# A hybrid attention block on one core: the high parts of A's q are set down by transfers that ScalarE issues

## The chip, the core and the metric

The kernel runs on one core of a Trainium2 chip. The core has five engines that run side by side, each in the order of its own queue: TensorE (PE in the profile) multiplies matrices, VectorE (DVE), ScalarE (ACT) and GpSimd (POOL) work elementwise, and SyncE (SP) does nothing here but issue transfers (DMAs). SP and ACT each have a queue from which transfers can be issued; the transfers themselves run on the DMA engines. Engines wait for one another, and for transfers, on semaphores. The metric is the device time of one execution in microseconds (us); lower is better. The time quoted is the median of three runs.

## What is computed

One transformer block in float32, 1024 tokens of width 1024. Its token-mixing half, cut to what matters:

```python
proj = h @ w_in[l]
qa = partial_rope(proj[..., :o1].reshape(b, s, A_Q_HEADS, HEAD_DIM), cos, sin)
ka = partial_rope(proj[..., o1:o2].reshape(b, s, A_KV_HEADS, HEAD_DIM), cos, sin)
...
oa = banded_attention(qa.reshape(b, s, A_KV_HEADS, A_GROUP, HEAD_DIM), ka, va,
                      A_WINDOW - 1, sink=sink_a[l])
...
ob = dilated_mixture_attention(qb, kb, vb).reshape(b, s, B_W).astype(x.dtype)
mixed = jnp.concatenate([rms_norm(oa, g_mix_a[l]), rms_norm(ob, g_mix_b[l])], axis=-1)
y = mixed @ w_out[l]
```

Mixer A has 8 query heads of 64 in two groups of 4, each group with one key and one value head, a window of 128 and a sink. Mixer B has 8 heads with three dilated windows each. An MLP of width 4096 follows.

## The kernel before

Matrix products that need float32 accuracy are made from parts: a number is split into a high part (rounded to a format that TensorE takes fast) and a low part (what is left), and three products are added (lines 861, 862 and 864 for the projections). So each projection result is split after it is computed, and both parts are stored.

**Projections.** There are six groups `u`: 0 and 1 are mixer A's (4 query heads, 1 key head, 1 value head each), 2 to 5 are mixer B's. Each is computed for two halves `x` of 512 tokens and three chunks `c` of 128 columns. `evac` (lines 734 to 844) takes a finished chunk out of PSUM: ACT writes the high part into a staging tile `hl` (line 763 after the rotary embedding on DVE in lines 757 to 760, or line 774), and DVE or POOL writes the low part beside it (line 766 or 777). The columns are laid out (`PARTS_A`, `PARTS_B`) so that the rows of a chunk belong to several heads interleaved. Transfers from SBUF to SBUF then set the rows down where TensorE needs them (line 803): keys into `kt`, queries into `qt`. In mixer A the high parts of q go to partitions 0 to 63 of `qt` and the low parts to partitions 64 to 127, in separate transfers (`s_` is 0 or 1), while a transfer of k carries both parts to both places (`both`). For each of the four pairs of `u` and `x` in mixer A that is 2 transfers for k, 5 for q's high and 5 for q's low parts. In mixer B it is q whose transfers carry both parts and k that is split.

**Scores.** Mixer A's items run per block of 128 queries: line 1177 multiplies `qt` and `kt` into `s_ps`, DVE adds the mask and finds the maximum (1192), ACT takes exponentials (1197), DVE the reciprocal (1201), ACT or POOL scales the rows (1207, 1209), TensorE transposes (1234), ACT and DVE split the transposed weights (1241, 1245), TensorE multiplies by the values (1269), ACT and DVE take the result out (1304, 1309) and SP stores it (1314). The values come by `vt` (825), a transpose (831) and `v_hl` (839, 842). Between these, TensorE computes the next projections.

**Buffers.** `hl` tiles come from a ring of five staging slots, which the ada weights `wa_st` (line 994, consumed by POOL in lines 1005 to 1010) and the gates `gate_st` (1034, stored in 1050) use too. A tile in a slot is free when the last transfer that reads it has landed. Weights of the projections come by `w_st` (530) and are split by ACT (539) and DVE or POOL (544). A rope table is made through `ptab` (719) and `tab` (721).

**Order.** Nothing here is scheduled by hand in the code's text. `Sched` (lines 175 to 313) is a list scheduler that runs while the program is built: each step carries an engine, a modelled duration, dependences, buffers it takes and gives, and a priority, and the step that can start first by the model is written out next. Where a step may run on two engines (`alts`), the one that would end first by the model gets it. For transfers the model keeps one clock of the DMA engines, `dma`, and counts 0.62 us of SP's time for each issue. Its clocks are estimates; on the chip the engines keep this order but run by their semaphores. All 533 transfers are issued by SP. Each transfer signals one of eight semaphores, given out in turn in the order in which the program was written, and in the compiled order a transfer waits for the one eight before it.

Of the kernel before, what the change touches and what calls it, by code (L numbers as in the profile page):

```python
# [148 lines left out]
PW = 0.0  # L149


class Ev:

    __slots__ = ("t", "eng")
# [20 lines left out]
class Sched:  # L175


    def __init__(self):
        self.clk = dict(PE=0.0, ACT=0.0, DVE=0.0, POOL=0.0, SP=0.0)
        self.queue = {e: [] for e in ("ACT", "DVE", "POOL", "SP")}  # L180
        self.pe = {}
        self.launch = []
        self.seq = 0
        self.dma = 0.0
        self.filler = None

    def step(self, dur, emit, deps=(), takes=(), gives=(), prio=5, after=None, kind="", n=1):
# [25 lines left out]

    def ready(self, o, e):
        t = 0.0
        for d in o.deps:
            if d.t is None:
                return None
            x = d.t + lat(d.eng, e)
            if x > t:  # L220
                t = x
        for r, n in o.takes:
            if n == 0:
                continue
            if len(r.free) < n:
                return None
            x = sorted(r.free)[n - 1]
            if x > t:
                t = x
        return t  # L230

    def give_out(self, e, o, start):
        dur, emit = o.alts[e] if o.alts else (o.dur, o.emit)
        for r, n in o.takes:
            r.free.sort()
            del r.free[:n]
        emit()
        end = start + dur
        if e == "SP":
            self.clk[e] = start + 0.62 * o.n  # L240
            self.dma = max(self.dma, start + 1.1) + max(dur, 0.62 * (o.n - 1))
            end = self.dma + 0.8
        else:
            self.clk[e] = end
        o.ev.t = end
        o.ev.eng = e
        o.gone = True
        for r, n in o.gives:
            r.give(end, n, e)
        self.end = end  # L250
        if o.after:
            o.after()
# [96 lines left out]
def hybrid_block(ctx: ExitStack, tc: tile.TileContext, x, positions, w_ada, b_ada, g_attn_post, w_in, w_out,  # L349
                 g_mlp_post, w_up, w_down, consts, out):  # L350
    nc = tc.nc
    ctx.enter_context(tc.manual_schedule())
    V, A, G, T = nc.vector, nc.scalar, nc.gpsimd, nc.tensor
    x, out = x[0], out[0]
# [91 lines left out]
            return ring_r(name)  # L446
        return st.stgp.tile([P, 1024], F32, name=name, tag="stg")

    def load(emit, nbytes, deps=(), takes=(), prio=5, gives=(), after=None, n=1):
        return op("SP", nbytes / (345e3 if prio > -500 else 370e3), emit, deps, takes=takes, prio=prio, gives=gives, after=after, n=n)  # L450

    def rsqrt_mean(dst, src, dep):
        box = []
# [280 lines left out]
    def evac(u, x, c, get_ps, done, r_bank):  # L734

        isb = u > 1
        parts = (PARTS_B if isb else PARTS_A)[c]
        cs = slice(512 * x, 512 * x + 512)
        b = {}
        e_q.setdefault((u, x), [])  # L740
        e_k.setdefault((u, x), [])

        def posted():
            n_in[u, x] = n_in.get((u, x), 0) + 1
            if n_in[u, x] == 3:
                st.posted += 1

        def f_new():
            b["f"] = stage("hl")[:].rearrange("p (s t) -> p s t", s=2)
            b["t"] = b["f"].bitcast(F32R)  # L750

        if c == 0:
            def f_rope():
                f_new()
                ps, t = get_ps(), b["f"][:, 1]
                cos, sin = tabs[0][:, cs], tabs[1]
                V.tensor_tensor(t[64:128], ps[0:64], sin[0:64, cs], ALU.mult)
                V.tensor_tensor(t[0:64], ps[64:128], sin[64:128, cs], ALU.mult)
                V.tensor_tensor(ps[:], ps[:], cos, ALU.mult)
                V.tensor_tensor(t, t, ps[:], ALU.add)  # L760
            e0 = e_rot[u, x] = op("DVE", 4 * t_dv(512), f_rope, [done] + e_tab[x], takes=[(r_stg, 1)],
                                  gives=[(r_bank, 1)], prio=2)
            eh = op("ACT", t_sb(512), lambda: A.copy(b["t"][:, 0], b["f"][:, 1]), [e0], prio=2)

            def f_lo(eng):
                return lambda: eng.tensor_tensor(b["t"][:, 1], b["f"][:, 1], b["f"][:, 0], ALU.subtract)
            el = op(("DVE", "POOL"), (t_dv(512), t_ptt(512)), (f_lo(V), f_lo(G)), [eh], prio=2)
        elif parts:
            n = P if c < 2 else parts[-1][1]
            sc_ = scl[0] if isb else None  # L770

            def f_hi():
                f_new()
                A.mul(b["t"][:n, 0], get_ps()[:n], -0.125 if sc_ is None else sc_[:n])

            def f_lo():
                V.scalar_tensor_tensor(b["t"][:n, 1], get_ps()[:n], -0.125 if sc_ is None else sc_[:n],
                                       b["f"][:n, 0], ALU.mult, ALU.subtract)
            eh = op("ACT", t_ps(512) + AP_COST, f_hi, [done, e_rot[u, x]], takes=[(r_stg, 1)], prio=2)
            el = op("DVE", t_dv(512) + AP_DV, f_lo, [eh], gives=[(r_bank, 1)] if c < 2 else [], prio=2)  # L780

        if parts:
            for whose in ("k", "q") if c == 0 else ("q", "k"):
                mine = [a for a in parts if a[3] == whose]
                if not mine:
                    continue
                both = isb == (whose == "q")
                nh = 2 if isb else 4 if whose == "q" else 1
                for s_ in ((0, 1) if not both else (None,)):
                    new = c == 0 and whose == "k" and s_ in (0, None)  # L790

                    def f_st(s_=s_, new=new, mine=mine, whose=whose, nh=nh, both=both):
                        if new:
                            if not x:
                                ks[u] = kring.tile([P, 2, 1024], F32R, name="kt", tag="kt")
                            qs[u, x] = qring.tile([P, 4, 512], F32R, name="qt", tag="qt")
                        dst = qs[u, x][:] if whose == "q" else ks[u][:, :, cs]
                        for p0_, n_, step, _, row in mine:
                            src = b["f"][p0_:p0_ + (n_ - 1) * step + 1:step]
                            m_ = n_ // nh  # L800
                            for i in range(2) if both else (s_,):
                                o = dst[64 * i + row:64 * i + row + m_].bitcast(F32)
                                nc.sync.dma_start(o, src if both else src[:, s_])  # L803
                    if new:
                        e_new[u, x] = Ev()
                    last = (whose == ("q" if c == 0 or not isb else "k")) and s_ in (1, None)

                    def after(new=new, last=last):
                        if new:
                            e_new[u, x].t = 0.0  # L810
                        if last and c < 2:
                            posted()
                    by = sum(a[1] * 2048 * (4 if both else 1) for a in mine)
                    e = load(f_st, by, [eh if s_ == 0 else el] + ([] if new else [e_new[u, x]]),
                             takes=[(r_k, 1 - x), (r_q, 1)] if new else [], prio=-12, n=len(mine) * (2 if both else 1),
                             gives=[(r_stg, 1)] if last else [], after=after)
                    (e_q if whose == "q" else e_k)[u, x].append(e)
        if c < 2:
            return
        nh = 2 if isb else 1  # L820
        o = P - 64 * nh

        def f_vt():
            b["vt"] = prp.tile([P, 512], F32, name="vt", tag="vt", bufs=1)
            A.copy(b["vt"][:64 * nh], get_ps()[o:])
        e = op("ACT", t_ps(512), f_vt, [done] + ([el] if parts else []), takes=[(r_vt, 1)], gives=[(r_bank, 1)], prio=2)

        def f_pv():
            b["pv"] = px.tile([P, 4, 64 * nh], F32, name="pv", tag="x")
            for j in range(4):  # L830
                T.transpose(b["pv"][:, j], b["vt"][:64 * nh, j * P:(j + 1) * P], ident[:64 * nh, :64 * nh])
        e = pe_op("post", 0.43, f_pv, [e], takes=[(r_x, 1), (r_v, 1)], gives=[(r_vt, 1)])

        def part(s_):
            return vs[u, x][:, :, :nh, s_], b["pv"][:].rearrange("p j (h d) -> p j h d", h=nh)

        def f_vh():
            vs[u, x] = vring.tile([P, 4, 2, 2, 64], F32R, name="v_hl", tag="v")
            A.copy(*part(0))

        def f_vl():
            V.tensor_tensor(part(1)[0], part(1)[1], part(0)[0].bitcast(F32), ALU.subtract)
        e = op("ACT", t_ps(256 * nh), f_vh, [e], prio=2)
        op("DVE", t_dv(256 * nh), f_vl, [e], gives=[(r_x, 1)], prio=2, after=posted)
# [1230 lines left out]
```

## Time and profile before

| what | value |
|---|---|
| median of 3 runs | 1166.8 us (1165.25 to 1167.23) |
| the profiled execution's own time | 1161.99 us |
| its span in the profile | 1160.2 us |
| mean granted clock of TensorE | 0.986 |
| DVE, ACT, POOL busy | 70%, 55%, 23% of the span |
| DMA traffic | 185.31 MB, mean 160 GB/s |

The profile is of one execution. In its rows, `out<-in` are the program's names for what an instruction writes and reads, `xcount` is a number of instructions, and `[5.51 <-DMA kt<-hl]` says that the engine stood idle for 5.51 us before the instruction and what came last of what it waited for. A row of windows lists the busy time of each engine within the window, then TensorE's granted clock (1.00 is full speed), the share of the DMA engines that was busy, and the GB/s. `SPq` and `ACTq` are issue queues; a row of them says how long the issuing took, not the transfer. A row of waits gives the engine, its line, what it waited for, and the sum in us, the count and the longest.

### The profile page before, as it was taken

Reading aid. Unit: us, or ns where it says so; the run is one execution under the profiler, and the core shown is the slowest. Engines: PE = TensorE matmul, PEld = TensorE weight load, DVE = VectorE, ACT = ScalarE, POOL = GpSimd, SP = SyncE. Lnnn points to the kernel's source line nnn. Section 1 sums busy time; section 2 is a strip of 40 time slices with the busy share of each in tenths; the row PEclk is TensorE's granted clock in tenths of the full one; section 3 lists DMA queues with packets and bytes.
Section 4 is the critical chain, followed back from the end, with each engine's and each line's share of the span. In section 5 each row is a group of like instructions: output and inputs, shape, how many; then the busy total and the mean of one; then the engine's idle time right before and its main releaser. Section 6 shows DMA issues by size and latency. Waiting matters only on the chain.

```text
span 1160.2 us, 15646 instructions
## 1 busy us (share of the span) xinstructions
PE 1117.1 (96%) x5416; PEld 926.6 (80%) x5416; DVE 815.4 (70%) x1380; ACT 639.2 (55%) x1105; POOL 261.1 (23%) x344
## 2 busy tenths in 40 slices
PE   8989989999999899998999999999999999999996
PEld 7768778788888787887788888888888888888885
DVE  7848576566666775658969665499653796547998
ACT  7949676455555774667676524563233732246542
POOL 2347667566663441112000000000000000000002
PEclk9989989999999989999999999999999999999998
DMA  9477857465545614554683057812369212585103
GB/s 351 161 174 168 168 120 182 111 153 122 134 102 130 156 48 139 193 181 182 257 314 118 19 207 274 315 50 89 120 220 326 106 55 73 184 306 181 37 19 146
DMA packets 90944, 185.31 MB, mean 160 GB/s; under 512 B 8432, under 2 KB 31088, under 8 KB 90864
## 3 DMA queue, kind: packets, MB, share of 16 engines
q1 hardware_dynamic: 90864, 184.30, 51.1%
q8 instruction: 43, 0.70, 0.3%
q14 instruction: 37, 0.30, 0.1%
HBM read 137.08 MB, written 28.31 MB: 143 GB/s over the span
## 4 chain that ended last, share of the span: by engine, by line
PE 70%; DVE 10%; DMA 7%; issue 4%; POOL 4%; ACT 3%; SPq 2%; DVEq 0%; POOLq 0%; ACTq 0%
PE mlp_ps L1898 16%; PE mlp_ps L1899 16%; PE mlp_ps L1897 16%; PE pj L861 3%; PE pj L864 3%; PE pj L862 3%; PE s_ps L1122 2%; PE o_ps L1257 1%; DMA wa<-in_w_ada 1%; SPq L803 1%; PE pt_ps L1227 1%; DMA wa_st<-in_w_ada 1%; DVE hw L1668 1%; PE pt_ps L1230 1%; PE s_ps L1177 1%
## 5 line engine op out<-in xcount | busy, mean ns | idle before, releaser
L1897 PE MATMUL mlp_ps<-hw 128*128 128x512 f32 x896 | 349.7, 390 | 1.2 <-ACT hw L1659 1.2
L1898 PE MATMUL mlp_ps<-hw 128*128 128x512 f32 x896 | 348.7, 389 | 1.1 <-DVE hw L1665 1.1
L1899 PE MATMUL mlp_ps<-hw 128*128 128x512 f32 x896 | 348.6, 389 | 0.0
L1897 PEld LDWEIGHTS mlp_ps<-hw 128*128 128x128 f32 x896 | 168.2, 188 | 36.8 <-ACT hw L1659 1.6
L1898 PEld LDWEIGHTS mlp_ps<-hw 128*128 128x128 f32 x896 | 168.2, 188 | 36.8 <-DVE hw L1665 1.4
L1899 PEld LDWEIGHTS mlp_ps<-hw 128*128 128x128 f32 x896 | 168.2, 188 | 34.9
L1668 DVE TENSOR_TENSOR hw<-w,hw 128x1024 fp32r<-128x1024 f32 x96 | 114.5, 1219 | 94.7 <-ACT hw L1661 94.4
L1661 ACT CAST hw<-w 128x1024 fp32r<-128x1024 f32 x96 | 97.5, 1047 | 129.8 <-PE mlp_ps L1899 97.5
L1997 POOL TENSOR_TENSOR st<-st,nhalf 128x1 f32<-128x1 f32 x8 | 7.8, 978 | 601.9 <-DVE st L1995 601.9
L861 PE MATMUL pj<-hw,w_hl 128*128 128x512 f32 x240 | 104.2, 434 | 0.0
L864 PE MATMUL pj<-hw,w_hl 128*128 128x512 f32 x240 | 95.5, 398 | 0.0
L862 PE MATMUL pj<-hw,w_hl 128*128 128x512 f32 x240 | 95.3, 397 | 0.0
L1245 DVE TENSOR_TENSOR ph<-pt_ps,ph 128x512 fp32r<-128x512 f32 (+1 forms) x110 | 69.7, 648 | 36.0 <-ACT ph L1241 35.7
L1661 ACT CAST hw<-u 128x1024 fp32r<-128x1024 f32 x48 | 48.7, 1052 | 64.6 <-PE mlp_ps L1899 64.6
L1241 ACT CAST ph<-pt_ps 128x512 fp32r<-128x512 f32 (+1 forms) x110 | 59.5, 555 | 32.1 <-PE pt_ps L1230 27.0
L1668 DVE TENSOR_TENSOR hw<-u,hw 128x1024 fp32r<-128x1024 f32 x48 | 57.0, 1218 | 18.2 <-ACT hw L1661 18.2
L1148 ACT ACTIVATE p_sb<-p_sb,mn 128x128 f32<-128x128 f32 (+3 forms) x64 | 49.7, 777 | 36.3 <-DVE mn L1141 34.9
L1955 DVE TENSOR_TENSOR yacc<-yacc,mlp_ps 128x512 f32<-128x512 f32 x96 | 62.1, 681 | 3.3 <-PE mlp_ps L1899 3.3
L1153 POOL TENSOR_SCALAR p_sb<-p_sb,den 128x128 f32<-128x128 f32 (+3 forms) x64 | 49.0, 775 | 47.8 <-DVE den L1151 44.6
L1010 POOL TENSOR_TENSOR ada_acc<-ada_acc,wa_st 128x512 f32<-128x512 f32 x42 | 55.5, 1320 | 3.5
L864 PEld LDWEIGHTS pj<-hw,w_hl 128*128 128x128 f32 x240 | 45.6, 190 | 10.7
L1473 PE MATMUL y_ps<-hw,oh 128*128 128x512 f32 x128 | 51.7, 404 | 0.0
(205 smaller groups left out, 2010.6 us busy)
## 6 DMA issues: line engine op xcount, KB each, us to landing
hw<-s_dram SPq DMA_DIRECT2D x84, 512.0 KB
wa_st<-in_w_ada SPq DMA_DIRECT2D x32, 512.0 KB
w<-in_w_up SPq DMA_DIRECT2D x32, 512.0 KB
w<-in_w_down SPq DMA_DIRECT2D x32, 512.0 KB
s_dram<-hw SPq DMA_DIRECT2D x28, 512.0 KB
w_st<-in_w_in SPq DMA_DIRECT2D x36, 256.0 KB
x_sb<-in_x SPq DMA_DIRECT2D x16, 512.0 KB
wa<-in_w_ada SPq DMA_DIRECT2D x32, 256.0 KB
```

The costliest lines, as they stand in the source:

```text
L861: T.matmul(ps, w[:, 0, n], h[0], start=(k == 0), stop=False)
L862: T.matmul(ps, w[:, 1, n], h[0], start=False, stop=False)
L864: T.matmul(ps, w[:, 0, n], h[1], start=False, stop=(k == KC - 1))
L1010: G.tensor_tensor(ada.acc[:, :512], ada.acc[:, :512], wa[:, j], ALU.add)
L1241: A.copy(b["ph"][:, 0, :w], b["pt"][:, :w])
L1245: V.tensor_tensor(b["ph"][:, 1, :w], b["pt"][:, :w], b["ph"][:, 0, :w].bitcast(F32), ALU.subtract)
L1661: A.copy(out[j][0], flat(src[j]))
L1668: V.tensor_tensor(out[j][1], flat(src[j]), out[j][0].bitcast(F32), ALU.subtract)
L1897: T.matmul(ps[m][:], sh, mh, start=starts and k == 0, stop=False, **kw)
L1898: T.matmul(ps[m][:], sh, ml_, start=False, stop=False, **kw)
L1899: T.matmul(ps[m][:], sl, mh, start=False, stop=k == 3, **kw)
L1955: e = op("DVE", t_dv(512), lambda: V.tensor_tensor(y(), y(), ps[m][:], ALU.add), [e, ml.e_y[tb, n]], gives=gives, prio=1)
```

## The change

In mixer A, the transfers of q's high parts are issued by ACT (`nc.scalar`) and stand in its queue; those of q's low parts, of k, and all of mixer B's stay with SP. That is 5 transfers for each of the four pairs of `u` and `x`, 20 of 533. The planner gets them as steps of the engine ACT and of a new kind, "small", with a clock of their own for the DMA engines (`few`) and 0.5 us of ACT's time per issue. A second new kind, "bulk", and its `SLACK` are used by no step. Since the model's numbers change, the planner also writes out the steps around these transfers in another order.

```diff
+SLACK, ISSUE = 0.8, 0.5
...
-        self.dma = 0.0
+        self.dma = self.few = 0.0
...
     def ready(self, o, e):
         t = 0.0
+        late = SLACK if e == "ACT" and o.kind == "bulk" else 0.0
...
-        if e == "SP":
+        if e == "SP" and o.kind != "small":
             self.clk[e] = start + 0.62 * o.n
             self.dma = max(self.dma, start + 1.1) + max(dur, 0.62 * (o.n - 1))
             end = self.dma + 0.8
+        elif o.kind == "bulk":
+            self.clk[e] = start + ISSUE * o.n
+            self.dma = max(self.dma, start + 1.1) + dur
+            end = self.dma + 0.8
+        elif o.kind == "small":
+            each = 0.62 if e == "SP" else ISSUE
+            self.clk[e] = start + each * o.n
+            self.few = max(self.few, start + 1.1) + max(dur, each * (o.n - 1))
+            end = self.few + 0.8
         else:
             self.clk[e] = end
...
-    def load(emit, nbytes, deps=(), takes=(), prio=5, gives=(), after=None, n=1):
-        return op("SP", nbytes / (345e3 if prio > -500 else 370e3), emit, deps, takes=takes, prio=prio, gives=gives, after=after, n=n)
+    def load(emit, nbytes, deps=(), takes=(), prio=5, gives=(), after=None, n=1, q="SP", kind=""):
+        return op(q, nbytes / (345e3 if prio > -500 else 370e3), emit, deps, takes=takes, prio=prio, gives=gives, after=after,
+                  n=n, kind=kind)
...
                 for s_ in ((0, 1) if not both else (None,)):
+                    eng = nc.scalar if s_ == 0 and not isb else nc.sync
                     new = c == 0 and whose == "k" and s_ in (0, None)
...
-                                nc.sync.dma_start(o, src if both else src[:, s_])
+                                eng.dma_start(o, src if both else src[:, s_])
...
                     e = load(f_st, by, [eh if s_ == 0 else el] + ([] if new else [e_new[u, x]]),
                              takes=[(r_k, 1 - x), (r_q, 1)] if new else [], prio=-12, n=len(mine) * (2 if both else 1),
-                             gives=[(r_stg, 1)] if last else [], after=after)
+                             gives=[(r_stg, 1)] if last else [], after=after, kind="small" if eng is nc.scalar else "",
+                             q="ACT" if eng is nc.scalar else "SP")
```

In the two orders as built, ACT has 26 instructions more: the 20 transfers, and 6 of the row scalings of line 1207, which go to ACT instead of POOL's line 1209. DVE has 3 more (2 weight splits of line 544, 1 low part of line 766), POOL 9 fewer. TensorE's instructions are the same but for their order between its rows 316 and 767.

More of the change, by code (lines that the diff above doesn't have):

```diff
@@ L218, in ready @@
                 return None
-            x = d.t + lat(d.eng, e)
+            x = d.t + lat(d.eng, e) + late
             if x > t:
@@ L226, in ready @@
                 return None
-            x = sorted(r.free)[n - 1]
+            x = sorted(r.free)[n - 1] + late
             if x > t:
@@ L789, in evac, with f_st @@
                 for s_ in ((0, 1) if not both else (None,)):
+                    eng = nc.scalar if s_ == 0 and not isb else nc.sync
                     new = c == 0 and whose == "k" and s_ in (0, None)
-                    def f_st(s_=s_, new=new, mine=mine, whose=whose, nh=nh, both=both):
+                    def f_st(s_=s_, new=new, mine=mine, whose=whose, nh=nh, both=both, eng=eng):
                         if new:
```

## The prediction

> **What bounds the kernel now.** I read the busy shares first, then TensorE's waits in the stretch that the order of instructions shows to be touched, then windows around each wait.
>
> ```profile
> PE 1117.1 (96%) x5416; PEld 926.6 (80%) x5416; DVE 815.4 (70%) x1380; ACT 639.2 (55%) x1105; POOL 261.1 (23%) x344
> ```
>
> TensorE is busy for all but 43 of 1160.2 us. So the change can win only where TensorE stands still, or works at half clock. The two programs' orders agree before TensorE's row 316 of some 4,490 and after its row 767, which by the trace is 62 to about 225 us, the stage that projects and scores mixer A. Everything later keeps its order and only shifts. Columns of the next view: window, its length, busy us (instructions) of each engine, granted clock, share of the DMA engines, GB/s.
>
> ```profile
> 60.00:80.00 20.00, 17.48 (x82) 13.82 (x81) 7.83 (x12) 7.91 (x15) 10.75 (x12) 1.00 0.74 188
> 80.00:100.00 20.00, 17.00 (x94) 14.74 (x95) 14.82 (x55) 13.85 (x46) 11.04 (x21) 0.83 0.86 193
> 100.00:120.00 20.00, 19.49 (x114) 16.14 (x113) 17.18 (x47) 17.79 (x51) 16.37 (x27) 1.00 0.70 156
> 120.00:140.00 20.00, 20.00 (x112) 16.48 (x111) 12.76 (x40) 15.31 (x44) 15.26 (x34) 1.00 0.80 165
> 140.00:160.00 20.00, 14.98 (x83) 12.81 (x82) 11.41 (x36) 13.00 (x38) 14.33 (x20) 0.83 0.36 85
> 200.00:220.00 20.00, 17.48 (x93) 14.55 (x92) 9.88 (x28) 8.18 (x18) 11.91 (x14) 0.91 0.51 127
> ```
>
> Three holes, each with a lower clock. The waits and the timeline name them:
>
> ```profile
> PE s_ps L1177 <- DMA kt<-hl: 5.5, 1, 5.5
> PE pv L831 <- ACT tab L721: 5.0, 1, 5.0
> PE pv L831 <- DVE ot L1293: 2.5, 1, 2.5
> ...
> 83.00 1.94 PE L1177 MATMUL s_ps<-kt,qt 128*128 128x128 f32 x8 [5.51 <-DMA kt<-hl]
> 148.71 0.69 PE L831 MATMUL pv<-head,vt 64*128 64x64 f32 x4 [5.02 <-ACT tab L721]
> 207.70 1.12 PE L831 MATMUL pv<-head,vt 128*128 128x128 f32 x4 [2.52 <-DVE ot L1293]
> ```
>
> I call them S1 (77.5 to 83.0), S2 (143.7 to 148.7) and S3 (205.2 to 207.7). The clock after the first two:
>
> ```profile
> 80.00:82.00 2.00, 0.00 (x0) 0.00 (x0) 0.60 (x1) 0.00 (x0) 0.00 (x0) 0.73 0.97 203
> 82.00:84.00 2.00, 1.00 (x5) 1.03 (x6) 1.92 (x4) 0.00 (x0) 0.00 (x0) 0.50 0.59 144
> 86.00:88.00 2.00, 2.00 (x8) 1.09 (x7) 0.18 (x1) 1.11 (x6) 1.02 (x4) 0.56 0.76 160
> ...
> 148.00:150.00 2.00, 1.29 (x6) 1.08 (x7) 1.17 (x4) 2.00 (x8) 1.92 (x3) 0.50 0.44 124
> 152.00:154.00 2.00, 2.00 (x14) 1.83 (x13) 1.66 (x7) 1.28 (x4) 1.92 (x5) 0.85 0.65 242
> ```
>
> After S1, TensorE works from 83.0 to about 87.7 at half clock: half of 4.7 us, 2.3 us, is lost besides the 5.5. After S2 it is 148.7 to 152.6, so 2.0 us. S1 costs 7.8 us in all and S2 7.0. S3 costs 2.5 and, by the mean clock of 0.91 over 20 us, about 1.8 more.
>
> **S1: what its scores wait for.** SP issues the kt and qt transfers of two halves back to back:
>
> ```profile
> 67.47 1.78 SPq L803 DMA_DIRECT2D kt<-hl  x2
> 69.31 8.35 SPq L803 DMA_DIRECT2D qt<-hl  x10
> 77.75 1.32 SPq L803 DMA_DIRECT2D kt<-hl  x2
> 79.16 7.46 SPq L803 DMA_DIRECT2D qt<-hl  x10
> ...
> 78.45 4.46 DMA kt<-hl
> ```
>
> The first score matmul depends, in the compiled order, on the first ten qt transfers. The last is issued at 77.06 (the 8.35 us end at 77.66), and the scores start at 83.0. The chain gives a landing: a kt issued at 77.75 is in at 78.45 + 4.46 = 82.91, so issue to landing is 5.2 us.
>
> The change gives 5 of these 10 to ACT, so two engines issue at once. Held by nothing else, SP would be through its 7 in 7 x 0.7 us, at 72.4 instead of 77.7. But every transfer waits, in the compiled order, for the semaphore of the one eight before it, whichever engine issued that. With at most 8 under way for 5.2 us each, one can land every 0.65 us; SP alone makes one every (77.66 - 67.47) / 12 = 0.85 us in the first half, and 0.74 in the second. So there is a little to gain, not half. The last two of SP's qt wait for the second kt and for ACT's second qt. That kt is issued about 68.6 as now (the last 0.6 of the 1.78 us), lands at 73.8, and the last qt, one issue later at 74.4, lands at 79.6; the scores could start at 79.7 at best. At worst the transfers are bound by the DMA engines (share 0.97 at 80 to 82) and all lands as now, 83.0. The share before that is lower,
>
> ```profile
> 72.00:74.00 2.00, 2.00 (x11) 1.62 (x10) 0.00 (x0) 0.00 (x0) 1.92 (x3) 1.00 0.64 103
> 76.00:78.00 2.00, 1.49 (x7) 0.91 (x5) 0.00 (x0) 0.59 (x1) 0.00 (x0) 1.00 0.68 168
> ```
>
> so neither end is nearer, and I take the middle, 81.3.
>
> Against this stands a reordering. The new plan puts the scores after 6 matmuls of the next projection instead of 18. Twelve matmuls at 0.23 us (their starts below) are 2.7 us of cover that now comes behind the scores, so TensorE stops at 74.8.
>
> ```profile
> 76.42 0.39 PE L864 MATMUL pj<-hw,w_hl 128*128 128x512 f32 x1
> 76.64 0.39 PE L861 MATMUL pj<-hw,w_hl 128*128 128x512 f32 x1
> ```
>
> Idle then is 81.3 - 74.8 = 6.5 us against 5.5: S1 counts +1.0, with bounds 79.7 - 74.8 - 5.5 = -0.6 and 83.0 - 74.8 - 5.5 = +2.7. Its half clock counts as it does now.
>
> The Trainium skill, "DMA: Bandwidth & Descriptors" (Issuing engines are not separate DMA queues), says that transfers started by several engines interleave on the same 16 DMA engines, and that a second issuer saves only sequencer time. The share of 0.97 agrees with it and the 0.64 does not. By that rule alone S1 would count its upper bound, and the sum below would be 1.7 us higher.
>
> **S2: a staging slot.** The high part of a projection takes a staging slot that an older one must have left:
>
> ```profile
> 144.02 0.59 ACT L774 ACTIVATE hl<-pj 64x512 fp32r<-64x512 f32 x1 [4.94 <-DMA qt<-hl]
> 144.52 0.61 ACT L539 CAST w_hl<-w_st 128x512 fp32r<-128x512 f32 x1
> ...
> 135.32 8.68 DMA qt<-hl
> ```
>
> The slot's last qt transfer is issued at 135.3, behind an ada weight load, and lands at 144.0. ACT stands from 139.1, and the weight split, vt, a score's exp and the rope table that wait behind it reach TensorE at 148.7. In the new order, the same instruction (now L788) takes another slot, that of gate_st, whose store to DRAM was issued long before:
>
> ```profile
> 131.83 0.34 SPq L1050 DMA_DIRECT2D gate_d<-gate_st  x1
> ```
>
> Its landing can't be later than 131.83 + 8.68 = 140.5, the slowest transfer seen here. What waits for the qt slot now is SP's next ada load, which ACT does not depend on. TensorE also has a dozen matmuls more (2.7 us) ahead of the scores of that half, which now need that instruction's low part. If it starts at 139.1 to 140.5 as its slot allows, the low part and its transfer (5.2 us) land at about 147, near when TensorE comes there. So I take S2's 7.0 us away and put 1.5 us back for what is late next, those scores; bounds 0 and 5.0 (a hole as long as the old).
>
> S3 hangs on an o_dram store and is outside of the moved instructions; it counts 0, with bounds -4.3 (gone, since arrival times shift) and 0.
>
> **ACT's added work.** Twenty issues, and six L1207 scalings that the planner now gives to ACT instead of POOL. An issue on ACT isn't in this trace; the nearest row is SP's:
>
> ```profile
> L803 SPq DMA_DIRECT2D qt<-hl x72: 547/610/1570, 69.3 to 384.5; - x72
> L1207 ACT ACTIVATE p_sb<-p_sb,den x18: 492/498/515, 96.0 to 167.7; 128x256 f32<-128x256 f32 x18
> ```
>
> That is 20 x 0.61 = 12.2 us, and 6 x 0.42 (four in 1.69 us back to back in the timeline) = 2.5:
>
> ```profile
> 132.56 1.69 ACT L1207 ACTIVATE p_sb<-p_sb,den 128x256 f32<-128x256 f32 x4
> ```
>
> Ten issues fall into 62 to 90 us, where ACT idles at least 30% of the time, and five lie between 120 and 147, where it idles 4.7 us before 140. They are free while that idling lasts, else 0.61 us each. Five issues (3.1) and the scalings (2.5) fall near 100 to 120, where ACT idles only 2.2 us: 5.6 - 2.2 = 3.4 us don't fit. TensorE can fill some of it with projection matmuls; bounds 0 and 3.4, taken 1.5. What SP gains, 20 x 0.61 us, has no price: nothing but S1 and S2 waits for its issuing. POOL's lighter load and the three more on DVE hide behind TensorE.
>
> **Sum.** +1.0 - 7.0 + 1.5 + 0 + 1.5 = -3.0 us. The profiled execution took 1161.99 us (span 1160.2) and would take 1159.0. It lies 4.8 us under the median of the three runs, 1166.8, so the predicted time is 1163.8.
>
> **Rivals.** *Slower: ACT's queue stands on transfers.* ACT runs in order, and its issues wait for SP's transfers eight before (the first burst for the masks, the ada load and a kt), and it has exps and evacuations queued behind them. Place: the third burst, 96 to 116 us, where ACT hasn't any slack. An issue that comes right after its eighth predecessor waits up to 5.2 us for it, and so do the exps; DVE, POOL and the scores follow. It decides once two such waits last together more than the 2.2 us of idle time and the filler's few matmuls. Price: 5.0 for a hole like S2's, 2.0 for its clock, 3.4 for the work: 10.4 + 1.0 - 5.5 = +5.9, 1172.7. For it: ACT's 17.79 of 20. Against it: in that stretch the transfer eight before is often much older. In SP's queue today such waits are rare (median issue 610 ns, longest 1,570).
>
> *No difference.* The transfers are bound by the DMA engines and land no earlier, so S1 grows by 2.7: 2.7 - 5.5 + 1.5 = -1.3, 1165.5. For it the DMA share of 0.97; against it 0.64. It decides if the first scores start at 83.0 as before. The Trainium skill's rule named above would have it so.
>
> *All holes shrink.* S1 at its lower bound, S2 gone with nothing behind it, S3 gone, no cost on ACT: -0.6 - 7.0 - 4.3 = -11.9, 1154.9. For it: ACT's idle time in most windows. Against it: three independent gains at once.
>
> *The change does nothing.* The eight semaphores, shared by both queues, keep the pace at 0.65 us whoever issues, and only the plan differs; then S1 counts +2.7 and the time is that of no difference, in whose chance it is.
>
> **Chances.** Forecast (S2 gone, S1 a little worse) 0.42; all shrink 0.10; no difference 0.14; slower 0.34. Two runs of this kernel differ by about 0.2%, 2.3 us, which is the bound of no difference. So faster 0.52, same 0.14, slower 0.34. The range goes from the case of all holes to the slower rival: 1155 to 1173. The forecast's own goes by S1's, ACT's and the scores' bounds from 1159.2 (-1.6 - 1.5 - 1.5) up to 1164.5, where no difference begins.
>
> **What would show it.** Right: TensorE's first L1193 waits 4.9 to 8.2 us and starts at 79.7 to 83; no wait over 3 us in 140 to 155 with the clock at 1.00 there; L788 near 139 without a wait for a qt; ACT below 19 of 20 in 100 to 120 with TensorE above 19. Wrong: ACT rows with long waits for DMA between 90 and 140, a first score later than 84, or a new hole of 4 us or more between 95 and 200.

## The result, and the profile after

| | median | range | ratio to before, 95% interval |
|---|---|---|---|
| before | 1165.16 us (15 runs) | 1162.52 to 1168.67 | |
| after | 1170.38 us (15 runs) | 1167.05 to 1175.81 | 1.0048 [1.0033, 1.0062] |

The changed kernel is slower, by some 5 us. Its profiled execution took 1170.36 us (span 1168.4). The one of before, 1161.99, lies 3.2 us under its median, so the two traces differ by more than the two kernels do: TensorE's last matmul starts 8.8 us later. The times inside the traces are told with that in mind.

The change does what it says: among the groups of the profile after there is one of 20 transfers issued by ACT (ns of one issue: least, median, most; first and last start). An issue takes it 0.64 us, where SP's row of before had 0.61:

```profile
L818 ACTq DMA_DIRECT2D qt<-hl x20: 599/643/1197, 66.0 to 150.6; - x20
```

The timeline's rows of TensorE with its four longest waits between 60 and 240 us, after. The line numbers are those of before plus 14 to 16:

```profile
76.09 0.46 PE L847 MATMUL pv<-head,vt 64*128 64x64 f32 x4 [4.81 <-ACT vt L841]
82.75 1.41 PE L1193 MATMUL s_ps<-kt,qt 128*128 128x128 f32 x8 [1.67 <-DMA qt<-hl]
100.71 1.84 PE L1250 MATMUL pt_ps<-head,p_sb 128*128 128x128 f32 x4 [4.22 <-POOL p_sb L1225]
209.20 0.38 PE L1273 MATMUL o_ps<-ph,v_hl 128*128 128x256 f32 x1 [3.34 <-ACT ph L1257]
```

S2, the old hole at 144, is gone. S1 is split in two. A hole at 96.5 to 100.7 is new, and the one near 207 is longer and waits for another engine. The windows after show S2 gone (140 to 160) and where the clock fell:

```profile
100.00:120.00 20.00, 19.29 (x97) 16.26 (x98) 11.16 (x34) 13.22 (x38) 12.85 (x26) 0.83 0.44 94
140.00:160.00 20.00, 19.42 (x107) 15.06 (x106) 11.74 (x34) 16.30 (x44) 17.14 (x34) 1.00 0.66 185
...
78.00:80.00 2.00, 2.00 (x6) 1.58 (x5) 0.00 (x0) 0.35 (x2) 0.00 (x0) 0.52 0.65 154
...
102.00:104.00 2.00, 2.00 (x11) 1.93 (x10) 0.79 (x2) 1.08 (x3) 1.92 (x3) 0.50 0.25 75
```

To see where time is lost and won, count TensorE's matmuls in both traces in order of their starts, from 0, and set the n-th against the n-th. Two of these pairs, the 900th and the last, before and then after:

```profile
187.69 0.40 PE L864 MATMUL pj<-hw,w_hl 128*128 128x512 f32 x1
...
1149.68 0.39 PE L1899 MATMUL mlp_ps<-hw 128*128 128x512 f32 x1
```

```profile
191.61 0.40 PE L880 MATMUL pj<-hw,w_hl 128*128 128x512 f32 x1
...
1158.46 0.39 PE L1915 MATMUL mlp_ps<-hw 128*128 128x512 f32 x1
```

| matmul number | 400 | 480 | 680 | 720 | 900 | 1200 | 1500 | last |
|---|---|---|---|---|---|---|---|---|
| after minus before, us | +1.6 | +10.0 | +11.5 | +5.1 | +3.9 | +7.6 | +8.5 | +8.8 |

So the changed kernel is 11.5 us behind just ahead of S2 and wins 6.4 there. From the 900th to the 1200th another 3.7 us go, in the hole near 207. Each has its rows.

**The new hole at 100.** TensorE's transposes wait for POOL's scaling of four rows (L1225). POOL's rows after, and then the same stretch before:

```profile
96.02 0.69 POOL L1025 TENSOR_SCALAR wa_st<-wa_st,cond 128x512 f32<-128x512 f32 x1 [8.35 <-DMA wa_st<-in_w_ada]
...
100.18 1.84 POOL L1225 TENSOR_SCALAR p_sb<-p_sb,den 128x256 f32<-128x256 f32 x4
...
165.53 1.29 POOL L780 TENSOR_TENSOR hl<-hl 128x512 fp32r<-128x512 f32 x1
...
185.72 0.69 POOL L1021 TENSOR_SCALAR ada_acc<-wa_st,cond 128x512 f32<-128x512 f32 x1 [10.22 <-DMA wa_st<-in_w_ada]
```

```profile
91.82 1.85 POOL L1209 TENSOR_SCALAR p_sb<-p_sb,den 128x256 f32<-128x256 f32 x4
93.64 0.70 POOL L1009 TENSOR_SCALAR wa_st<-wa_st,cond 128x512 f32<-128x512 f32 x1
...
178.68 0.69 POOL L1005 TENSOR_SCALAR ada_acc<-wa_st,cond 128x512 f32<-128x512 f32 x1 [0.24 <-DMA wa_st<-in_w_ada]
```

Before, the scalings stand ahead of an ada piece in POOL's queue; after, behind it. That piece waits 8.35 us for its weights, whose load SP issued at 86.5 behind the second burst, and the scalings, which need none of it, wait along.

**The hole at 207.** SP's rows after and before, and the chain of waits after:

```profile
86.53 2.45 SPq L1010 DMA_DIRECT2D wa_st<-in_w_ada  x2
...
166.99 1.24 SPq L1330 DMA_DIRECT2D o_dram<-ot  x2
169.00 1.22 SPq L818 DMA_DIRECT2D qt<-hl  x2
...
178.37 0.38 SPq L1010 DMA_DIRECT2D wa_st<-in_w_ada  x1
```

```profile
160.50 1.30 SPq L803 DMA_DIRECT2D kt<-hl  x2
161.90 1.19 SPq L803 DMA_DIRECT2D qt<-hl  x2
163.54 1.27 SPq L1314 DMA_DIRECT2D o_dram<-ot  x2
...
171.90 0.38 SPq L994 DMA_DIRECT2D wa_st<-in_w_ada  x1
```

```profile
170.96 7.39 DMA qt<-hl
178.37 7.20 DMA wa_st<-in_w_ada
...
201.37 5.97 DMA w_st<-in_w_in
...
207.42 0.63 ACT w_hl L553
```

In the new order a pair of o_dram stores stands ahead of the second kt transfer and two qt transfers of B's first half, and the low part that these carry went from DVE (L766 before) to POOL (L780, at 165.53, behind four scalings). So the first two qt leave at 169.0 instead of 161.9 (not all of it by the order: TensorE is 5 us behind at that point anyway); an ada load waits for a later one (170.96 + 7.39, so 178.37), POOL idles 10.22 us for it, and everything behind its ada pieces is late: a weight split, the slot that it frees, the next weight load, ACT's split at 207.42. Neither hole waits directly for a transfer that ACT issued. The first two runs ask whether ACT's issuing plays a part all the same.

### The profile page after: what moved, and what is told of

Its sections match the earlier page's. It is cut to its first block, busy times and chain, and to the rows that moved or that the text cites. A ratio compares the mean times of both kernels' runs of the same rounds, so it can differ in the third digit from the quotient of the medians.

```text
span 1168.4 us, 15634 instructions
## 1 busy us (share of the span) xinstructions
PE 1123.5 (96%) x5416; PEld 929.3 (80%) x5416; DVE 818.1 (70%) x1383; ACT 639.4 (55%) x1111; POOL 255.5 (22%) x335
## 4 chain that ended last, share of the span: by engine, by line
PE 68%; DVE 10%; DMA 8%; issue 5%; ACT 4%; POOL 4%; SPq 0%; ACTq 0%; DVEq 0%; POOLq 0%
PE mlp_ps L1914 16%; PE mlp_ps L1913 16%; PE mlp_ps L1915 16%; PE pj L877 3%; PE pj L880 3%; PE pj L878 3%; PE s_ps L1138 2%; DMA qt<-hl 2%; PE o_ps L1273 1%; DMA wa<-in_w_ada 1%; DMA w_st<-in_w_in 1%; PE pt_ps L1243 1%; DVE hw L1684 1%; PE pt_ps L1246 1%; DMA kt<-hl 1%
## 5 line engine op out<-in xcount | busy, mean ns | idle before, releaser
L878 PE MATMUL pj<-hw,w_hl 128*128 128x512 f32 x240 | 96.5, 402 | 0.0
L880 PE MATMUL pj<-hw,w_hl 128*128 128x512 f32 x240 | 96.5, 402 | 0.0
```

The source lines that it names most:

```text
L878: T.matmul(ps, w[:, 1, n], h[0], start=False, stop=False)
L880: T.matmul(ps, w[:, 0, n], h[1], start=False, stop=(k == KC - 1))
```

## Experiments

| run | median, us | ratio to before, 95% interval |
|---|---|---|
| new order, SP issues all | 1173.63 | 1.0066 [1.0043, 1.009] |
| old order, ACT issues | 1164.57 | 0.9991 [0.9972, 1.0009] |
| after, three issues behind `vt` | 1167.0 | 1.0018 [1.0001, 1.0035] |
| after, POOL scales first | 1170.27 | 1.004 [1.0016, 1.0064] |
| after, stores last | 1165.42 | 1.0003 [0.9968, 1.0037] |
| after, both of these | 1165.71 | 1.0002 [0.9976, 1.0028] |
| old order, ACT issues the fourth pair's | 1167.75 | 1.001 [0.9986, 1.0034] |
| old order, ACT issues all but the third's | 1165.84 | 0.9992 [0.9965, 1.0019] |
| the same, gate load behind `o_sb` | 1158.53 | 0.9952 [0.9935, 0.997] |
| before, gate load behind `o_sb` | 1164.92 | 1.0001 [0.9988, 1.0014] |

**Order and issuer apart.** The change does two things: it lets ACT issue, and it makes the planner write out another order. The first run keeps after's order and lets SP issue all:

```diff
-                                eng.dma_start(o, src if both else src[:, s_])
+                                nc.sync.dma_start(o, src if both else src[:, s_])
```

> The changed kernel's order, but SP issues all transfers. Theory A (the engines' order): the loss sits in the new order itself, above all in POOL, which stands at an ada load ahead of row scalings (96.5 to 100.7 us in the changed kernel), and in the 12 matmuls moved behind the first scores; the transfers land no earlier or later whoever issues them. Then the first scores start at 82 to 84 us after one idle piece of about 8 us, POOL's hole stays near 4 us, and the time is within 2 us of the changed kernel's 1170. Theory B (ACT's queue): the loss comes from ACT, which stands on a transfer eight back in front of vt (TensorE idle from 71.3 to 76.1). Then that hole goes and the time falls by 5 us or more, to 1165 or below.

The second keeps before's order and lets ACT issue:

```diff
-                                nc.sync.dma_start(o, src if both else src[:, s_])
+                                (nc.scalar if s_ == 0 and not isb else nc.sync).dma_start(o, src if both else src[:, s_])
```

> The order of before, but ACT issues the high parts of A's q. Theory A: no POOL hole, the first scores start at about 83 us as in before, and the time is within 2 us of before (1165). Theory B: ACT's waits for transfers make it slower by about 5 us (1170).

TensorE's rows in the first (new order, SP alone), and then in the second (old order, ACT issues):

```profile
81.47 1.94 PE L1193 MATMUL s_ps<-kt,qt 128*128 128x128 f32 x8 [6.92 <-DMA qt<-hl]
99.36 1.83 PE L1250 MATMUL pt_ps<-head,p_sb 128*128 128x128 f32 x4 [3.37 <-POOL p_sb L1225]
...
210.22 0.58 PE L1273 MATMUL o_ps<-ph,v_hl 128*128 128x256 f32 x1 [3.89 <-ACT ph L1257]
```

```profile
81.59 1.08 PE L1177 MATMUL s_ps<-kt,qt 128*128 128x128 f32 x8 [3.05 <-DMA kt<-hl]
...
103.62 0.74 PE L1177 MATMUL s_ps<-kt,qt 128*128 128x256 f32 x4 [2.14 <-DVE mn L1192]
...
148.77 0.46 PE L831 MATMUL pv<-head,vt 64*128 64x64 f32 x4 [0.92 <-ACT tab L721]
```

The order alone makes the kernel slower, with the same holes at 100 and 210, and in that order SP alone gets the first scores going at 81.47, earlier than with ACT's help (82.75). The issuing alone leaves the time as it was, within the interval, and in its trace S1 and S2 are shorter (3.0 and 0.9 us, 5.5 and 5.0 before). So the loss is the order's. Where the second run spends what it wins at S1 and S2 comes further down.

**S1's split.** In the profile after, ACT's copy L841 into `vt` stands 8 us behind four issues. The last three go behind that copy:

```profile
75.45 0.58 ACT L841 COPY vt<-acc 64x512 f32<-64x512 f32 x1 [8.03 <-DMA qt<-hl]
```

```diff
-                                eng.dma_start(o, src if both else src[:, s_])
+                                go = partial(eng.dma_start, o, src if both else src[:, s_])
+                                if eng is nc.scalar and (u, x) == (0, 0) and c:
+                                    held.append(go)
+                                else:
+                                    go()
...
             A.copy(b["vt"][:64 * nh], get_ps()[o:])
+            while held:
+                held.pop(0)()
```

> The changed kernel, with the last three of ACT's five transfers of the first burst put behind the vt copy in ACT's queue. Theory A with the transfers bound by the DMA engines: TensorE's 4.8 us wait for vt shrinks below 1.5 us, but the first scores still start at 82 to 84 us, so the idle time is only moved, POOL's hole stays, and the time is within 2 us of 1170. Theory B: 5 us faster, 1165.

```profile
85.18 1.94 PE L1199 MATMUL s_ps<-kt,qt 128*128 128x128 f32 x8 [10.88 <-DMA qt<-hl]
```

The wait for `vt` went, and the scores came 2.4 us later with one hole of 10.88. So the idle time at S1 doesn't come from the stand in ACT's queue: TensorE has to wait for the q data either way. The median is 3.4 us under after's, with an interval that meets after's at the edge. The profiled execution (1170.32 us, span 1168.5) is as long as after's, so the trace can't show where that would come from. Whether the stand costs anything in the end stays open.

**The hole at 100 by itself.** POOL's ada piece goes behind the four scalings:

```diff
         def f_acc():
+            if i == 1:
+                ada.late = [f_acc2]
+            else:
+                f_acc2()
...
                     G.tensor_scalar(p, p, d, 1.0, ALU.mult, ALU.mult)
+                    while h == 3 and ada.late:
+                        ada.late.pop()()
```

> The changed kernel, with POOL's first ada piece after the first (its second wa_st tile) put behind the four row scalings that follow it in POOL's queue. Theory A: the 4.2 us wait of TensorE at 100.7 us falls below 1 us and the half clock behind it (102 to 107 us) with it: 4.2 + 2 = 6 us faster than the changed kernel, 1164. Theory B: within 2 us of 1170.

```profile
104.22 2.69 PE L1259 MATMUL pt_ps<-head,p_sb 128*128 128x128 f32 x8 [2.26 <-POOL p_sb L1232]
```

A miss. The hole at 100.71 is gone, but one of 2.26 us stands at the next transposes; the 900th matmul starts at 188.06, 3.6 us earlier than after's, and the last one is still 2.8 us earlier. But this execution took 1167.44 us, 2.8 under the run's median, and the median is that of after. By the medians nothing is won at 100.

**The hole at 207 by itself.** The low part of that half goes back to DVE, right behind ACT's high part, and the pair of stores waits until the half's transfers are issued:

```diff
+                if (u, x) == (2, 0):
+                    V.tensor_tensor(b["t"][:, 1], b["f"][:, 1], b["f"][:, 0], ALU.subtract)
...
+                        if (u, x, c) == (2, 0, 0):
+                            st.hold = whose == "k"
+                            while st.wait and not st.hold:
+                                st.wait.pop(0)()
...
             def f_st():
+                if st.hold:
+                    st.wait.append(f_st2)
+                else:
+                    f_st2()
```

> The changed kernel, with two steps near 165 us put as before's order has them: the low part of mixer B's first k and q goes to DVE instead of POOL, and the pair of o_dram stores that stands ahead of the second kt in SP's queue goes behind that half's qt. Theory C: the hole of 3.3 + 0.9 us near 209 comes from there: kt and qt leave late and in one bunch (168.3 to 175 us), the next ada load waits for them (POOL idle 10.2 us to 185.7), and behind POOL's ada pieces the weight splits. Then the second kt leaves by 166.5, POOL's wait falls to 6 us or less, the hole to 2.5 us or less, and the time by 2 to 4 us to about 1167. Rival: the weights are late for another reason (the DMA engines), the hole stays, and the time is within 1.5 us of 1170.

SP's and POOL's rows, and TensorE's, of this run:

```profile
163.20 1.30 SPq L825 DMA_DIRECT2D kt<-hl  x2
164.60 1.19 SPq L825 DMA_DIRECT2D qt<-hl  x2
165.96 1.26 SPq L1347 DMA_DIRECT2D o_dram<-ot  x2
```

```profile
179.94 0.69 POOL L1032 TENSOR_SCALAR ada_acc<-wa_st,cond 128x512 f32<-128x512 f32 x1 [5.47 <-DMA wa_st<-in_w_ada]
```

```profile
210.21 0.66 PE L858 MATMUL pv<-head,vt 128*128 128x128 f32 x4 [2.62 <-DVE ot L1320]
```

POOL's wait falls from 10.22 to 5.47, TensorE's hole is again the one of before (2.52 there), and the median is 5.0 us under after's, level with before. So moving these few instructions takes the loss away; which of the two, the low part or the stores, was not tried apart. The forecast's gain isn't there: this trace is 10.5 us behind before at the 680th matmul, wins 6.4 at S2 as after does, and is 4.1 behind at the 720th (before's own trace being 3.2 us under its median), so S1 and the hole at 100 take about what S2 gives. With POOL's edit added, the expectation and the result:

> The edits of the last kernel and of the one that puts POOL's row scalings first, together in the changed kernel. Theories A and C: both holes shrink, 5 to 8 us faster than the changed kernel, 1163 to 1166, about the time of before; what is left of the order's cost is the 12 matmuls moved behind the first scores, against the gain at 144 to 152. Rival: the holes only move on, 1168 or more.

1165.71: the hole at 100 comes back as 3.19 us at 105.2, and nothing more is won. It is also the second run with the edit at 165 that is level with before.

**Keeping the old order.** If issuing costs nothing and shortens S2, why was the second run no faster? Two runs gave ACT only some of the issues, the fourth pair's (`u` and `x` both 1), and all but the third pair's:

```diff
-                                nc.sync.dma_start(o, src if both else src[:, s_])
+                                (nc.scalar if s_ == 0 and (u, x) == (1, 1) else nc.sync).dma_start(o, src if both else src[:, s_])
```

> The order of before; ACT issues only the high parts of the last of the four bursts (group 1, second half), 5 transfers, the rest SP. The 5.0 us hole at 144 to 149 and its half clock (2.0) came from a staging slot whose transfers stood in SP's queue behind an ada load. If ACT's queue frees them, the hole falls to 1 us as it did with all four bursts on ACT (0.9), without ACT's added load at 96 to 116: 4 to 7 us faster than before, 1159 to 1161. Rival: the hole goes only with the timing of all four; then within 2 us of 1165.

```diff
-                                nc.sync.dma_start(o, src if both else src[:, s_])
+                                (nc.scalar if s_ == 0 and not isb and (u, x) != (1, 0) else nc.sync).dma_start(o, src if both else src[:, s_])
```

> The order of before; ACT issues the high parts of three bursts, and SP those of the third (group 1, first half), which falls where ACT is saturated. If ACT's added work there is what the kernel with all four bursts on ACT gave back (a wait of 2.1 us for DVE at 103.6), that wait falls below 1 us and the time is 2 to 3 us below that kernel's 1164.6: about 1162. Rival: no difference from it, 1164 to 1165.

Neither was faster. In the first of them S2 fell to 0.95 us, but S1 came out at 6.62; in the second the wait at 103.6 is gone, and the 1500th matmul starts at 295.82, 2.7 us ahead of before. It is all lost at 413, by the hole and a half clock behind it, and the first has a hole of 3.30 us at the same place. TensorE's, POOL's and SP's rows of the second:

```profile
413.32 0.80 PE L1473 MATMUL y_ps<-hw,oh 128*128 128x512 f32 x1 [2.57 <-ACT oh L1431]
```

```profile
404.90 2.38 POOL L1357 TENSOR_TENSOR hw<-wo_st,hw 128x1024 fp32r<-128x1024 f32 x1
```

```profile
407.31 0.33 SPq L1372 DMA_DIRECT2D gate_a<-gate_d  x1
407.74 0.38 SPq L1418 DMA_DIRECT2D o_sb<-o_dram  x1
```

With these issuers the gate's load waits for POOL's last split of `w_out`, which ends at 407.28, and the first o_sb load, which TensorE needs, stands behind the gate's load in SP's queue. Before, and in the second run, where ACT issues for all four pairs, the gate's load waits for an earlier split by ACT (before: gate 403.28, o_sb 406.12). That its tile got another place among the buffers is the likely reason, but the traces don't show places.

The second run, in which ACT issues for all four pairs, spends its gain elsewhere. ACT's row:

```profile
101.47 0.58 ACT L1304 COPY otmp<-o_ps 64x512 f32<-64x512 f32 x1 [3.45 <-DMA qt<-hl]
```

ACT stands 3.45 us at two issues of the third pair, DVE waits for this copy, and TensorE for DVE (the 2.14 us at 103.62 above). From the 400th to the 480th matmul that trace loses 4.9 us against before; with the third pair's transfers on SP it loses none there. Another 3.9 us go between the 1200th and the 1500th, where TensorE waits 2.61 us at 260.54 for a scaling on POOL.

The last edit exchanges the gate's and the o_sb load; POOL writes one column of the gate's tile first, which is meant to keep the tiles where they are:

```diff
+        def f_gate():
+            G.memset(ph2.gate[:, :1], 0.0)
+            ph2.held.append(1)
+        ph2.e_gate = load(f_gate, 524288, [e_mod[0], e_mod[1]], prio=-7)
...
+            if ph2.held:
+                ph2.held.clear()
+                nc.sync.dma_start(ph2.gate[:], gate_d[0][:])
```

> The kernel before, its order, with ACT issuing q's high parts of the first, second and fourth pair of mixer A (SP those of the third, as in the run before this one), and with the load of the gate put behind the first load of o_sb in SP's queue (POOL writes one column of the gate's tile first, so that it keeps its place). Theory (the gain up to 400 us is real and was given back because that gate load, which stood behind POOL's split of w_out, held the o_sb load up): o_sb is issued at about 403 to 405 instead of 407.74, the wait of TensorE's L1473 at 413 (2.6 us) is gone, and the time is 2 to 4 us under the kernel before, about 1162. Rival (TensorE has fixed points further on, or the gain at 400 us is chance): the hole at 413 goes and others take its place, and the time is that of before, 1165.

> Control: the kernel before, all transfers issued by SP, with the same exchange of gate load and first o_sb load. There the gate load is not held up, so both theories expect no change: 1165 with an interval that holds 1, no hole of 2 us at 405 to 420.

SP's rows, and TensorE's at S2 and at its end, of the first; then TensorE's of the control:

```profile
403.36 0.38 SPq L1423 DMA_DIRECT2D o_sb<-o_dram  x1
407.27 0.33 SPq L1426 DMA_DIRECT2D gate_a<-gate_d  x1
```

```profile
146.66 0.46 PE L831 MATMUL pv<-head,vt 64*128 64x64 f32 x4 [2.19 <-ACT tab L721]
...
1146.37 0.39 PE L1907 MATMUL mlp_ps<-hw 128*128 128x512 f32 x1
```

```profile
148.45 0.68 PE L831 MATMUL pv<-head,vt 64*128 64x64 f32 x4 [3.91 <-ACT tab L721]
...
1152.83 0.39 PE L1907 MATMUL mlp_ps<-hw 128*128 128x512 f32 x1
```

The hole at 413 is gone and the gain stays: 1158.53 us, 0.5% faster than before and the fastest here. The control is at before's time, so what separates the two is the issuers alone, and no execution of the one is as slow as the fastest of the other (at most 1162.87 and at least 1162.96). ACT's issuing of 15 transfers is worth some 6 us here, once neither the planner's order nor the gate's load takes it back. By the two traces 4.2 of 6.5 us come at S2, between the 680th and the 720th matmul, where the hole is shorter and the clock stays full behind it. Another 2 us come only past the 2700th, where both run the same instructions: each has a hole of 3 us at about 545, and the granted clock in 545 to 550 is 0.68 in the control and 1.00 in the other. That part is chance by these two traces.

## Why the prediction was wrong

The forecast was 3 us faster; it came out some 5 us slower. The time lies within the range that was given, near the price of the slower rival, but that is luck: it came from steps that rival didn't have.

- *S1, +1.0, bounds -0.6 and +2.7.* Mis-sized. The idle time is nearly as forecast: 4.81 + 1.67 = 6.5 us, and the scores start at 82.75, inside 79.7 to 83. But they start only 0.25 us earlier than before with 12 matmuls (2.8 us) fewer done, so S1 has cost 2.5 by then: the split hole halves the clock twice, at 76 to 80 too. The half clock behind the scores is shorter for it, and at the 400th matmul 1.6 is left. The data come no earlier in this trace, as the rival of no difference had it. In this order SP alone was even earlier (81.47). In the old order the first scores start at 81.1 to 82.7 with ACT's help, and at 83.0, 83.2 and 84.0 without, which is 0.3 to 2.9 us. The rule of the Trainium skill's "DMA: Bandwidth & Descriptors" (Issuing engines are not separate DMA queues), that a second issuer saves only sequencer time, agrees with both: five issues at SP's 0.61 us are 3.1 us. The prediction read it too strictly when it put S1 at its upper bound by it.
- *S2, 7.0 away and 1.5 put back.* Right: 6.4 us won net, where 5.5 was forecast. L788 stands at 138.80 without a wait for a qt, no wait over 3 us is left in 140 to 155, and the clock is 1.00.
- *ACT's added work, +1.5, and the slower rival.* In the new order ACT is busy 13.22 of 20 us in 100 to 120, where it was 17.79 before, and the time is lost without ACT's issuing too, so the rival isn't the cause. But its mechanism is real. In the old order ACT stands 3.45 us on transfers at 101, in the third burst, as the rival had it, and 4.9 us go there. Its net there is still nothing, by the gains at S1 and S2: that run is at 0.9991 [0.9972, 1.0009].
- *The step that failed* is "S3 hangs on an o_dram store and is outside of the moved instructions; it counts 0". Matmuls 900 to 1200 lost 3.7 us, at and around S3. By the two traces TensorE's own order differs only from 70 to 165 us in the kernel before (the prediction's 62 to 225 is too wide), so S3's matmuls were indeed not moved. But what they wait for hung on a pair of stores and a low part at about 165 us that were: putting these two back won 5.0 us.
- *Its companion*, "POOL's lighter load and the three more on DVE hide behind TensorE", looked at how much POOL has to do and not at the order of it. The hole at 100 (4.22 us, and after it a clock of 0.50) is a scaling behind an ada piece whose weights are late. The run with POOL's scalings first took the wait at 100.71 away, which shows its cause, but didn't bring the time back, so its price at the end isn't shown.

Put together: S1 and the hole at 100 took about what S2 gave, and S3's loss is what remains. The reordering was known, and the working followed the order only at the two old holes. The sign written under "wrong", a new hole of 4 us or more between 95 and 200, is the one that came true.

## What to carry to other kernels

When a change goes through a planner, price the new order and not the edit: walk each engine's queue through the whole touched stretch and ask of every pair that swapped what now stands behind a load or a store that is late. Run the edit in the old order and the new order without the edit; here the first came out level and the second cost it all. When an engine with work of its own issues transfers, ask which issue stands on an older transfer and what is queued behind it: giving one pair of four back to SP took a stand of 3.45 us away. And when a gain vanishes further on, look there for a load that waits for a buffer ahead of one that is urgent: exchanging two loads turned a change without effect into a gain of 0.5%.

## What the runs showed of the hardware

ACT's median issue took 0.64 us, yet it stood idle for 8.03 us ahead of its copy at 75.45, behind four of them. The two engines' transfers share eight semaphores, so an issue on one engine waits for a landing of the other's: in the trace after, ACT's issue at 74.77 signals the same semaphore as a kt that SP issued at 67.34, and that kt's landing is complete at 74.70.

A hole of 3 us doesn't settle the clock. Windows behind S1, of the old order with ACT's issues (a hole of 3.05) and of the same without the third pair's (3.16), there behind S2 as well (2.11); the granted clock is the third number from the end:

```profile
83.00:85.00 2.00, 1.51 (x10) 0.92 (x8) 1.93 (x10) 1.20 (x2) 1.01 (x1) 1.00 0.62 106
```

```profile
83.00:85.00 2.00, 2.00 (x6) 1.50 (x5) 1.19 (x9) 0.88 (x3) 1.41 (x2) 0.50 0.58 120
...
147.00:149.00 2.00, 2.00 (x12) 2.00 (x11) 1.07 (x5) 0.22 (x1) 1.83 (x5) 0.50 0.39 75
```

About the same length left the clock at full in one and at half in the other, and the shortest halved it too, while a hole of 2.19 at S2 in the fastest kernel left it at 1.00 in 147 to 149. By S1's and S2's half clock in the trace of before, that is worth some 2 us a hole. The Trainium skill, "TensorE: Matmul & The Clock Gate" (Part 1: The HAM clock gate), says that the gate falls back after at least one idle window of about 3.4 us, and that these windows run freely and don't start with the kernel. That it hangs on where a hole falls agrees with these rows. If an idle window is one without any work, the hole of 2.11 us doesn't agree: it is shorter than a window and halved the clock.
